# Add and GELU on one core: the first load of y cut into a narrow and a wide piece

## The chip, the cores and the metric

The kernel runs on one core of one Trainium2 chip. The metric is the device time of one execution in microseconds (us). The kernel before takes 120.14 us (median of three runs, 120.08 to 120.14).

## The reference

```python
batch, dim = 1024, 4096            # x and y, float32
z = x + y
out = 0.5 * z * (1 + tanh(sqrt(2/pi) * (z + 0.044715 * z**3)))   # float32
```

Each of x, y and the output has 16.78 MB, so 33.55 MB are read from HBM (the chip's main memory) and 16.78 MB are written to it. Nothing is used twice.

## The kernel before, in words

Each of the three tensors is seen as 128 partitions by 32768 columns (`xv`, `yv`, `ov`, L91). One partition holds eight whole rows of the tensor, which lie together in HBM, so a DMA over a range of columns moves one unbroken run of bytes per partition: 8192 columns make a run of 32 KB, 16384 columns one of 64 KB. In what follows such a run is called a row of the DMA.

Tile `z` (L120) holds all 32768 columns. The loads of x land in it, the sums overwrite them, the results overwrite the sums, and the stores leave from it. Loads of y go to tiles `y` of 8192 columns (`YS`), of which two buffers exist (`pool_y`, L115; taken in L131); a third y load must wait until the first buffer was read. `load_y` works out from a load's first column which tile it belongs to and where in it, and takes a new buffer only where that place is 0 (L129 to L131), so several loads may fill one tile.

The columns are worked on in 16 chunks of 2048 (`CH`). For chunk c there are four steps:

- `add` (L149): z = x + y, on VectorE (DVE) for chunks 0, 2, 4, 6, 8 and 12, on GpSimd (POOL) for the other ten.
- `mag` (L154): w = |z|, ScalarE (ACT), into one of two PSUM tiles.
- `gelu` (L157): w = gelu(-w), ScalarE.
- `end` (L166): z = max(z, 0) + w, VectorE.

All DMAs are issued by SyncE (SP), from one queue in a fixed order (L173):

```python
sp = [(load_y, 0), (load_x, 0), (load_y, 1), (load_x, 1), (load_y, 2), (load_y, 3)]
sp += [(store, i) for i in range(len(stores))]
```

The sizes, in columns, are `xloads = [16384, 16384]`, `yloads = [8192] * 4` and `stores = [16384, 10240, 6144]` (L96 to L99). The tile framework puts a wait in front of an issue where data or buffers ask for it: y load 2 waits for the adds of chunks 0 to 3, y load 3 for those of chunks 4 to 7, each store for the `end` steps of its columns. The first four loads wait for nothing.

`begin_early(nc, 2)` (L214) takes the first two DMAs of SP's queue and puts them ahead of the barrier with which the program starts; what stands behind them is issued after that barrier. `wait_late` (L215) rearranges the program's end so that the last store's completion is waited for late.

Of the kernel before, what the change touches and what calls it, by code (L numbers as in the profile page):

```python
# [66 lines left out]
def kernel(  # L67
# [26 lines left out]
    CH = 2048  # L94
    PS = 2
    xloads = [16384, 16384]  # L96
    yloads = [8192, 8192, 8192, 8192]
    FIRST = 8
    stores = [16384, 10240, 6144]  # L99

# [69 lines left out]
            ends.setdefault(c, ins.ins)  # L170


    sp = [(load_y, 0), (load_x, 0), (load_y, 1), (load_x, 1), (load_y, 2), (load_y, 3)]  # L173
    sp += [(store, i) for i in range(len(stores))]
    pool = [(add, c) for c in range(C) if c not in by_dve]
    dve, acts = [], []
# [69 lines left out]
```

## Time and profile before

| | |
|---|---|
| median of three runs | 120.14 us |
| span of the profiled execution, first to last instruction | 118.57 us (the page rounds to 118.6) |
| what lies around the span (120.14 less 118.57) | 1.57 us |
| DVE, ACT, POOL busy | 59.8, 60.8, 55.5 us (50, 51, 47%) |
| DMA packets' time, share of 16 engines' span | 98.6% |
| bytes moved | 50.33 MB, 424 GB/s over the span |
| first DMA issued; last DMA landed | 0.00 us; 118.53 us |

The page has no time of its own for the profiled execution besides the span; the table sets the span beside the median of the runs. The trace also records each DMA packet with its start, duration and size. A packet here is one row of a DMA; each of the 16 DMA engines carries 8 of the 128 rows of every DMA, and after them a packet of 4 bytes that counts up the semaphore.

### The profile page before, as it was taken

Reading aid. Unit: us, or ns where it says so; the run is one execution under the profiler, and the core shown is the slowest. Engines: PE = TensorE matmul, PEld = TensorE weight load, DVE = VectorE, ACT = ScalarE, POOL = GpSimd, SP = SyncE. Lnnn points to the kernel's source line nnn. Section 1 sums busy time; section 2 is a strip of 40 time slices with the busy share of each in tenths; the row PEclk is TensorE's granted clock in tenths of the full one; section 3 lists DMA queues with packets and bytes.
Section 4 is the critical chain, followed back from the end, with each engine's and each line's share of the span. In section 5 each row is a group of like instructions: output and inputs, shape, how many; then the busy total and the mean of one; then the engine's idle time right before and its main releaser. Section 6 shows DMA issues by size and latency. Waiting matters only on the chain.

```text
span 118.6 us, 160 instructions
## 1 busy us (share of the span) xinstructions
DVE 59.8 (50%) x24; ACT 60.8 (51%) x34; POOL 55.5 (47%) x14
## 2 busy tenths in 40 slices
DVE  0000000000399999699994594257999457742000
ACT  5000000000067979999379705797798999940000
POOL 0000000000399999997000029999999999100000
DMA  7989888998889988988899898998899889999996
GB/s 243 464 365 696 354 354 354 663 398 354 354 387 497 531 354 354 707 354 354 354 420 464 365 520 354 531 531 354 354 531 531 354 354 442 442 442 442 398 398 265
DMA packets 1296, 50.33 MB, mean 424 GB/s; under 512 B 144, under 2 KB 144, under 8 KB 144
## 3 DMA queue, kind: packets, MB, share of 16 engines
q1 hardware_dynamic: 1296, 50.33, 98.6%
HBM read 33.55 MB, written 16.78 MB: 424 GB/s over the span
## 4 chain that ended last, share of the span: by engine, by line
DMA 48%; POOL 34%; POOLq 4%; ACT 3%; DVE 2%; issue 0%; SPq 0%; DVEq 0%
POOL z L149 34%; DMA z<-in_x_dram 26%; DMA y<-in_y_dram 21%; POOLq L213 4%; DVE z L166 2%; ACT w L154 2%; ACT w L157 2%; SPq L132 0%; POOLq L149 0%; DVEq L166 0%
## 5 line engine op out<-in xcount | busy, mean ns | idle before, releaser
L149 POOL TENSOR_TENSOR z<-z,y 128x2048 f32<-128x2048 f32 x10 | 55.3, 5563 | 45.6 <-DMA z<-in_x_dram 31.1
L154 ACT ACTIVATE w<-z 128x2048 f32<-128x2048 f32 x16 | 30.1, 1880 | 42.5 <-DVE z L149 36.0
L166 DVE SCALAR_TENSOR_TENSOR z<-z,w 128x2048 f32<-128x2048 f32 (+1 forms) x17 | 36.4, 2157 | 16.0 <-ACT w L157 16.0
L149 DVE TENSOR_TENSOR z<-z,y 128x2048 f32<-128x2048 f32 x6 | 24.0, 4009 | 30.3 <-DMA z<-in_x_dram 30.1
L157 ACT ACTIVATE w<-w 128x2048 f32<-128x2048 f32 x16 | 29.8, 1862 | 0.5
L198 ACT ACT_TABLE_LOAD x1 | 1.3, 1283 | 1.3 <-PEq L230 1.3
L197 DVE MEMSET one<- 128x1 f32 x1 | 0.1, 59 | 1.3 <-PEq L230 1.3
L198 ACT ACTIVATE one<-one 128x1 f32<-128x1 f32 x1 | 0.2, 203 | 0.0
L230 POOL MEMSET const-float32-0.0<- 128x1 f32 x1 | 0.1, 98 | 0.2 <-issue 0.2
L230 POOL MEMSET const-bfloat16-1.0<- 128x1 bf16 x1 | 0.1, 101 | 0.0
L230 POOL MEMSET const-uint8-127<- 128x1 uint8 x1 | 0.1, 101 | 0.0
L230 POOL MEMSET const-float32-1.0<- 128x1 f32 x1 | 0.1, 98 | 0.0
## 6 DMA issues: line engine op xcount, KB each, us to landing
y<-in_y_dram SPq DMA_DIRECT2D x4, 4096.0 KB, 23.7
out_dram<-z SPq DMA_DIRECT2D x1, 5120.0 KB, 14.9
out_dram<-z SPq DMA_DIRECT2D x1, 3072.0 KB, 11.0
z<-in_x_dram SPq DMA_DIRECT2D x2, 44.9
out_dram<-z SPq DMA_DIRECT2D x1, 21.6
```

The source lines that it names most:

```text
L149: eng.tensor_add(out=zt[:, a:b], in0=zt[:, a:b], in1=yt[s][:, o : o + b - a])
L154: nc.scalar.activation(out=wt[c], in_=zt[:, a:b], func=act.Abs)
L157: nc.scalar.activation(out=wt[c], in_=wt[c], func=act.Gelu_apprx_tanh, scale=-1.0)
L166: ins = nc.vector.scalar_tensor_tensor(out=zt[:, a + o : a + o + n], in0=zt[:, a + o : a + o + n], scalar=0.0, in1=wt[c][:, o : o + n], op ...
L197: nc.vector.memset(one, 0.0)
L198: nc.scalar.activation(out=one, in_=one, func=act.Gelu_apprx_tanh)
L213: tc.compile()
L230: nc = _bacc.Bacc("TRN2", target_bir_lowering=False, num_devices=1)
```

## The change

The first load of y is made in two DMAs. The first carries columns 0 to 1023 (4 KB in each of 128 partitions, 0.5 MB), the second columns 1024 to 8191 (28 KB each, 3.5 MB). Both fill the same y tile. The order of the list on SP's queue stays otherwise the same; the other loads of y are numbered one higher.

```diff
     xloads = [16384, 16384]
-    yloads = [8192, 8192, 8192, 8192]
+    yloads = [1024, 7168, 8192, 8192, 8192]
     FIRST = 8
...
-    sp = [(load_y, 0), (load_x, 0), (load_y, 1), (load_x, 1), (load_y, 2), (load_y, 3)]
+    sp = [(load_y, 0), (load_y, 1), (load_x, 0), (load_y, 2), (load_x, 1), (load_y, 3), (load_y, 4)]
     sp += [(store, i) for i in range(len(stores))]
```

`begin_early(nc, 2)` is not changed. The two DMAs that it moves ahead of the barrier were the first y load and the first x load; now they are the two pieces of the first y load, and the first x load is issued behind the barrier. On the other engines every instruction stays, in the same order.

## The prediction

> **What bounds the kernel.** I read the page's DMA rows first, then the chain of waits, then the opening by windows and by the trace's single DMA packets.
>
> ```profile
> DMA  7989888998889988988899898998899889999996
> DMA packets 1296, 50.33 MB, mean 424 GB/s; under 512 B 144, under 2 KB 144, under 8 KB 144
> q1 hardware_dynamic: 1296, 50.33, 98.6%
> ```
>
> The 16 DMA engines are taken for 98.6% of the span, and no compute engine for more than 51%. The records of single packets say it more sharply: I followed each engine's 72 rows from the first to the last, and from one packet's end to the next one's start there is never more than 1 ns. The kernel is one unbroken DMA stream, so its end is the start of that stream, plus each engine's 3 MB at a fixed rate, plus a tail (the last packet ends at 118.07 us on the latest engine, the last semaphore counts at 118.53).
>
> The chain of waits shows why the compute work doesn't matter here although it names POOL for 34%:
>
> ```profile
> 0.43 30.92 DMA z<-in_x_dram
> ...
> 44.68 25.46 DMA y<-in_y_dram
> ```
>
> The 25.46 us of the third y load are mostly time behind the second x load, which lands at 60.4 us. SP issues every later DMA while an earlier one still moves: y load 2 at 44.7 us (x until 60.4), y load 3 at 57.9 (y load 2 until 70.1), the stores at 77.6, 96.3 and 107.6, with the DMA ahead landing at 79.9, 99.2 and 111.3. The smallest cover is 2.2 us, in front of the first store.
>
> So only two things can move the end: the time the stream takes per row, and its opening. The opening by windows (columns: busy time of DVE, ACT, POOL, granted clock, DMA share, GB/s; a packet is booked where it starts):
>
> ```profile
> 0.00:1.00 1.00, 0.00 (x0) 0.00 (x0) 0.20 (x4) 1.00 0.00 0
> 1.00:2.00 1.00, 0.06 (x1) 0.74 (x1) 0.00 (x0) 1.00 1.64 524
> 2.00:3.00 1.00, 0.00 (x0) 0.74 (x2) 0.00 (x0) 1.00 0.61 262
> 3.00:11.00 8.00, 0.00 (x0) 0.00 (x0) 0.00 (x0) 1.00 0.99 426
> ```
>
> 524 GB/s for 1 us are sixteen 32 KB rows, one per engine; a share of 1.64 means that they take 1.64 us on average. The next eight (262 GB/s) take 0.61 x 16 / 8 = 1.22 us, and in steady flow a row takes 1.21. The single records: first packets start between 1.019 and 1.951 us and take 2.135 (the earliest) to 1.214 us (the two latest, at 1.898 and 1.951). They end between 2.77 and 3.16. So the early starters lose up to 0.92 us in their first packet, the latest lose nothing, and each engine stays in the phase it then has. Second packets take 1.224 us on average, the worst 1.259; third ones 1.212.
>
> **The change, part by part.**
>
> *Eight more rows per engine.* The spacing of like packets is 908.3 ns for 24 KB, 1209.2 for 32 KB and 1510.3 for 40 KB. The slope is (1510.3 - 908.3) / 16384 = 0.03674 ns a byte, which leaves 908.3 - 903.0 = 5.3 ns per packet whatever its size. A row of 4 KB is then 155.8 ns, one of 28 KB 1058.8, together 5.3 more than one of 32 KB; eight rows make 43 ns. The extra DMA also adds one semaphore packet, 6 ns to the next packet's start. Sum in steady flow: +0.05 us. Nothing hides it, since the stream has no gaps.
>
> *The same in the opening.* All of the 4 KB rows run before about 3.2 us, where packets are slower. How a row of 4 KB behaves there no row shows. The lower end is the 5.3 ns of steady flow. The upper end for a switch to a fresh row is the worst second packet, 1.259 against 1.213: 46 ns. The mean excess of second packets is 1.224 - 1.213, 11 ns; but the end belongs to the slowest of 16 engines, not to the average. I take for that engine half of its eight switches at the worst and half at the mean: 4 x 46 + 4 x 11 = 228 ns. With the 49 ns above it is +0.28 us; the ends are +0.05 and 8 x 46 + 49 = +0.42 us.
>
> *Can the opening get shorter?* Shortening the first packet helps engines that lose time in it. But the engine that starts at 1.951 loses nothing (1.214 us against 1.213), and it alone carries the end: 1.951 plus the same 3 MB. A gain needs that latest start to move. The bound is the mean start of the 16 engines, 1.369 us: -0.58 us. A loss needs the slow flow to last: if the last engine ran its 32 KB of small rows as slowly as the slowest first packet, 2.135 instead of 1.214, that is +0.92 us.
>
> *The second piece of y behind the first.* It is issued where the first x load was, at 0.43 us. From issue to the engines the first DMA takes 1.02 to 1.95 us. With the same lag the second is 0.43 us behind the first on each engine, and the first piece keeps an engine busy for 8 x 0.156 = 1.25 us; 0.8 us to spare. If its lag is greater by more than that, the engines stand idle for the rest.
>
> *The first x load behind the barrier.* It takes the place of y load 1, at 1.26 us instead of 0.43; y load 1 and x load 1 move back by one issue (0.33 to 0.45 us), so the last of them ends by about 2.5 us. The first y tile keeps the engines busy to 11.24 us, so this costs nothing; without that cover it would be the 0.83 us of the later issue. Nothing else stands on SP between them, and POOL, DVE and ACT first wait for x at 31 us.
>
> *Waits.* The adds of chunk 0 now need two y semaphores instead of one, and y load 2's reuse of the buffer follows both; the x load that lands last (31.35 us, y at 12.0) still ends the wait. Behind that wait on SP stand y load 3 and the stores. If the stream moves, all of it moves alike, and the 2.2 us of cover stay.
>
> One rule speaks against a small DMA. The Trainium skill, "DMA: Bandwidth & Descriptors", section "Anatomy of one DMA — SWDGE (gpsimd) path", gives about 2.0 us fixed for each DMA; were it paid in the stream, the sum by it would be near 122.1 us. The trace differs: from the first y load's last row to the first x load's first row an engine loses 6 ns, so between queued DMAs such a cost isn't in the stream.
>
> The sum: 118.57 us of span + 0.28 + 1.57 around it = 120.42 us, against the median of 120.14. About 0.2% (0.24 us) is what a measurement of this kernel can tell from no change; the line runs through this forecast's band.
>
> **The rivals.**
>
> *Bookkeeping only, not slower.* The opening slows by time, not by row: all first packets end within 0.39 us of each other however early they began, which speaks for a common moment until which flow is thin. Then 32 KB in eight pieces meet the same moment as 32 KB in one, and only 0.05 to 0.15 us come on top: 120.19 us. Against it: second packets are still slow, by up to 46 ns, after that moment.
>
> *Faster.* The late starters are late because the early ones' long first packets stand before them. The spread of 0.93 us in starts, while only 16 rows flow, speaks for it; against it, the two latest run at full rate at once, beside engines that are at their slowest, and the number of rows in the first DMA stays at 128. If the latest start falls to between 1.6 and 1.37 us, the gain is 0.30 to 0.53 after the 0.05 of bookkeeping: 119.75 us at its middle. It decides from a latest start under 1.66 us.
>
> *Much slower.* The small rows are too short to cover what the opening asks of each fresh row, or the second piece reaches the engines late. Price between 0.42 and 0.97 us, in the middle 120.84 us. For it: the slowest first packet. Against it: the 0.8 us to spare, and the first x rows, fresh too, at 2.418 us like all later ones.
>
> *The change doing nothing* isn't a case of its own: two DMAs for one are in the program's order on SP.
>
> **How the numbers follow.** The forecast (+0.15 to +0.42) has 0.40, of which 0.12 falls under the line of 0.24 us and 0.28 over it. Bookkeeping only has 0.20, all of it the same. Faster has 0.24. Much slower has 0.16. So faster 0.24, same 0.12 + 0.20 = 0.32, slower 0.28 + 0.16 = 0.44. The range goes from 119.70, which leaves out the larger gains (about 0.08), to 120.95, which leaves out the larger losses (about 0.08) and leaves little for cases that I don't see. The forecast's own band is 120.29 to 120.56.
>
> **What would show it.** In the changed kernel's packets: sixteen rows of 4 KB starting near 1.02 to 1.95 us, as first rows did; on the latest engine, eight of them in about 1.48 us (8 x 0.156 + 0.23); no gap before the 28 KB rows; the first x row starting 0.28 us later than 11.25 to 11.65; and from there every landing later by the same amount. If the first x rows start within 0.1 us of before, the rival of bookkeeping holds; if earlier, the faster one; if there is a gap in front of the 28 KB rows, their late arrival. The forecast is wrong as a whole if the stream opens a gap anywhere behind the first x load, or if the time moves while the first x rows do not.

## The result, and the profile after

The changed kernel took 120.33 us (median of 21 runs, 120.12 to 120.64) against 120.12 us of the kernel before (21 runs beside it): ratio 1.0018, 95% interval 1.0011 to 1.0025. That is +0.21 us, against +0.28 forecast. Two later comparisons of the same code, on two chips, gave 0.9986 (0.9971 to 1.0001) and 0.9983 (0.9969 to 0.9997). By the medians those two differ from the kernel before by 0.04 and 0.07 us only; their ratios lie lower because 7 of the 29 and 7 of the 35 runs of the kernel before beside them took over 120.45 us, and none of the changed kernel's 12 and 12 did. The sign of so small a change did not hold from one set of runs to the next, and most of what follows rests on traces, where steps of 0.05 us within one trace can be seen.

The profiled run of the changed kernel took 120.16 us with a span of 118.67 us, 0.10 us over the span before. The page's DMA rows:

```profile
DMA  6999888998889988988899898998899889999996
DMA packets 1440, 50.33 MB, mean 424 GB/s; under 512 B 160, under 2 KB 160, under 8 KB 288
q1 hardware_dynamic: 1440, 50.33, 98.7%
```

There are 144 packets more (128 rows and 16 semaphore packets), the same bytes, and the stream is as full as before. The opening by windows, with the columns as before:

```profile
0.00:1.00 1.00, 0.00 (x0) 0.00 (x0) 0.20 (x4) 1.00 0.06 4
1.00:2.00 1.00, 0.06 (x1) 0.75 (x1) 0.00 (x0) 1.00 0.82 131
2.00:3.00 1.00, 0.00 (x0) 0.73 (x2) 0.00 (x0) 1.00 1.28 516
3.00:11.00 8.00, 0.00 (x0) 0.00 (x0) 0.00 (x0) 1.00 1.03 443
```

From 1 to 2 us 131 GB/s are 32 rows of 4 KB, which take 0.82 x 16 / 32 = 0.41 us on average, though one costs 0.156 in steady flow. Where only whole 32 KB packets could be seen before, the small rows now show when the opening is slow. By the trace's packets, sixteen first rows start between 0.996 and 1.702 us and take up to 1.031 us; rows that start between 2.0 and 2.5 us take 174 ns on average, and from 2.5 us on every one takes 159 (a packet's duration overlaps the next one's by 3). The 28 KB rows follow without a gap.

The chain of waits:

```profile
1.25 30.24 DMA z<-in_x_dram
...
44.85 25.42 DMA y<-in_y_dram
```

x load 0 is now issued at 1.25 us instead of 0.43 and still takes its turn in the stream; it lands at 31.49 instead of 31.35. From there every load lands 0.11 to 0.14 us later than before (41.20, 60.55, 70.27, 79.98), and the last store 0.10 us later (118.64).

### The profile page after: what moved, and what is told of

The parts are those of the page before. It is cut to its first block, busy times and chain, and to the rows that moved or that the text cites. A ratio compares the mean times of both kernels' runs of the same rounds, so it can differ in the third digit from the quotient of the medians.

```text
span 118.7 us, 162 instructions
## 1 busy us (share of the span) xinstructions
DVE 59.8 (50%) x24; ACT 60.8 (51%) x34; POOL 55.5 (47%) x14
## 4 chain that ended last, share of the span: by engine, by line
DMA 47%; POOL 34%; POOLq 4%; ACT 3%; DVE 2%; issue 0%; DVEq 0%
POOL z L149 34%; DMA z<-in_x_dram 25%; DMA y<-in_y_dram 21%; POOLq L213 4%; DVE z L166 2%; ACT w L154 2%; ACT w L157 2%; POOLq L149 0%; DVEq L166 0%
```

## The experiments

Theories: **switches** (the prediction's: each change to a fresh row costs extra while the opening is slow), **moment** (its first rival: the opening is slow until some moment, whatever the rows), and **order** (x load 0 behind the barrier is what costs). The edits are against the kernel before, where the heading doesn't name the changed kernel. The time shown is the median; the ratio is that to the kernel before on the same chip. It compares all runs of the two and lies near the ratio of their means, so it can differ from that of the medians by up to 0.15%.

**The changed kernel again.**

> The changed kernel once more, for a second trace of its opening. The theory of the prediction (every switch to a fresh row costs extra while the opening is slow): ratio 1.0015 to 1.0025, and 4 KB rows after an engine's first one that are visibly longer than 156 ns. The rival (the opening is slow until a moment, whatever the size of the rows): only an engine's rows before about 2 us are long, all later ones 156 ns, and the time is 0.05 to 0.15 us over the kernel before.

120.08 us, ratio 0.9986 (0.9971 to 1.0001). The slow-down didn't come back. In the trace only 4 of the 4 KB rows that start after 2 us take over 170 ns, and none that starts after 2.3 us, as *moment* has it. x load 0 lands at 31.43 us, 0.08 us later than in the first trace of the kernel before. The spread among engines is new: they have moved the first 32 KB between 2.50 and 3.26 us, where the kernel before needed 2.77 to 3.17. Most engines run ahead; the latest does not.

**The wide piece first.**

```diff
+    yloads = [7168, 1024, 8192, 8192, 8192]
+    sp = [(load_y, 0), (load_y, 1), (load_x, 0), (load_y, 2), (load_x, 1), (load_y, 3), (load_y, 4)]
```

> The same two pieces in the other order: 28 KB rows first, then 4 KB rows. The first x load still stands behind the barrier, and the number of rows and DMAs is that of the changed kernel. Theory (small rows cost in the opening): the small rows now run at about 10 us, so +0.05 us, ratio 1.0004. Rival (slow until a moment): +0.05 us as well. Third theory (it is the x load behind the barrier, or the second piece's issue, that costs): as the changed kernel, +0.2 us, ratio 1.0018.

120.18 us, 1.0001 (0.9982 to 1.0021): no cost to be told, which speaks against *order* at 1.0018, though the interval just reaches it. x load 0 lands at 31.49 us, as in the changed kernel, although the small rows now run at 10 us. That speaks against *switches*. The profiled execution took 120.56 us, and its landings show where the extra time sits: from x load 1 to the y load behind it 9.85 us pass and to the next one 9.89, against 9.70 and 9.72 in the kernel before. Summed over the rows that start from 35 to 82 us, an engine loses 0.57 us here against steady rows, and 0.06 in the first trace of the kernel before. That has nothing to do with the edit, as the later copies show.

**The split in the second tile.**

```diff
+    yloads = [8192, 1024, 7168, 8192, 8192]
+    sp = [(load_y, 0), (load_x, 0), (load_y, 1), (load_y, 2), (load_x, 1), (load_y, 3), (load_y, 4)]
```

> The split is made in the second load of y instead of the first; the first two DMAs are those of the kernel before. It has the rows and the semaphores of the changed kernel, but away from the opening: what the stream pays for rows alone. All theories: 8 x 5.3 + 6 ns, +0.05 us, ratio 1.0004. If it is as slow as the changed kernel (1.0018), the opening has no part in the cost.

120.15 us, 1.0002 (0.9985 to 1.0019). The trace gives the price far better than the time: from x load 0's landing to that of the split tile 41.171 - 31.400 = 9.771 us pass, against 9.726, 9.722 and 9.723 us in three traces of the kernel before. The split costs the stream +0.047 us in this one trace; 0.049 had been worked out. The same stretch without a split takes 9.705 to 9.726 us over all traces that have it, so the price is good to some 0.02 us.

**Eight small pieces in the first tile.**

```diff
+    yloads = [1024] * 8 + [8192, 8192, 8192]
+    sp = [(load_y, 0), ..., (load_y, 7), (load_x, 0), (load_y, 8), (load_x, 1), (load_y, 9), (load_y, 10)]
```

> The first tile of y is loaded by eight DMAs of 4 KB rows: 64 rows per engine instead of 8, and seven more DMAs. By the stream's own price 64 x 155.8 + 8 x 6 less 8 x 1209.2 + 6 ns: +0.34 us, ratio 1.0028. Rival (slow until a moment): just that. Theory (a switch costs extra in the opening): the first eight or sixteen of an engine's rows carry 0.23 us on top, +0.57 us or more, ratio 1.0047. If DMAs of small rows can't be issued as fast as they are carried out (1.25 us each), gaps show between them and the loss is greater.

121.83 us, 1.0132 (1.0107 to 1.0158): +1.6 us (120.12 x 0.0132; 1.7 by the medians), beyond all theories. The windows show where:

```profile
3.00:4.00 1.00, 0.00 (x0) 0.00 (x0) 0.00 (x0) 1.00 1.06 406
4.00:5.00 1.00, 0.00 (x0) 0.00 (x0) 0.00 (x0) 1.00 0.87 287
5.00:6.00 1.00, 0.00 (x0) 0.00 (x0) 0.00 (x0) 1.00 0.97 344
```

The eight DMAs land at 3.42, 4.65, 7.19, 8.47, 9.81, 11.12, 12.41 and 13.67 us. All spacings but one are 1.23 to 1.34 us; the third DMA takes 2.54. That is 1.29 us over the 1.25 of steady flow (8 x 0.156 + 0.006), and so most of what the eight cost beyond the 0.34 us worked out. It is the first one behind the barrier, issued at 1.26 us. From 4.0 to 4.5 us only 12.1 of the 16 engines have a packet in flight on average: some stand idle, over 2.7 us after that issue. So the prediction's last means of getting slower, a piece that reaches the engines late, is real; in the changed kernel it had no chance, since 28 KB rows stand behind the small ones. Rows of 200 to 1060 ns show until about 10.5 us, beside which SP was issuing until 7.5 us. Why the third DMA reaches the engines so late is not shown.

**The same eight in the second tile.**

```diff
+    yloads = [8192] + [1024] * 8 + [8192, 8192]
+    sp = [(load_y, 0), (load_x, 0), (load_y, 1), ..., (load_y, 8), (load_x, 1), (load_y, 9), (load_y, 10)]
```

> Eight DMAs of 4 KB rows again, now for the second tile of y, whose rows run at 31 to 41 us; the first two DMAs are those of the kernel before. In the first tile these eight cost 1.58 us instead of the 0.34 worked out from the steady stream. If that is the opening and the issues beside it, the second tile pays the stream's price, +0.34 us, ratio 1.0028, and all its rows take 156 to 160 ns. If rows of 4 KB in a longer row cost that much anywhere, ratio 1.013 again, and rows of 200 to 400 ns show among them.

120.63 us, 1.0037 (1.0024 to 1.0050). By the trace the tile lands 41.703 - 31.478 = 10.225 us after x load 0, +0.50 us against 9.724. That is more than the 0.34 of the steady price: 391 of the 1024 small rows take 160 to 219 ns instead of 159, which makes 0.14 us an engine. But it is less than a third of what the same eight cost in the opening. So the rest of their 1.6 us belongs to the opening and the issues beside it, not to 4 KB rows as such. Why a third of the rows are late here is open.

**x load 0 early again, in the changed kernel.**

```diff
-    begin_early(nc, 2)
+    begin_early(nc, 3)
```

> The changed kernel with three DMAs ahead of the barrier instead of two, so that the first x load is issued early again, right behind the two pieces of y. If the x load behind the barrier is part of the cost, the time falls from 1.0018 towards 1.0004. Theory of the prediction and the rival of a slow moment: no change against the changed kernel, 1.0005 to 1.0025, since the first tile of y covers the issue to 11 us; the barrier itself falls some 0.4 us later, which nobody waits for.

120.08 us, 1.0003 (0.9992 to 1.0015). x load 0 is issued at 0.89 us and lands at 31.45, inside the 31.43 to 31.49 of the changed kernel's three traces. *Order* falls: 0.36 us of earlier issue brought the landing no nearer.

**x load 0 before y load 0.**

```diff
+    sp = [(load_x, 0), (load_y, 0), (load_y, 1), (load_x, 1), (load_y, 2), (load_y, 3)]
```

> The kernel before with its first two DMAs exchanged: 64 KB rows of x first, then 32 KB rows of y. Rows, bytes and DMAs are the same, so the opening alone tells. Slow until a moment: ratio 1.0000, within 0.0005, and the first rows' excess over 2.418 us is as large as it was over 1.213 us. If the excess of the opening grows with the size of the first rows, up to 0.4 us slower (1.003); if fewer switches in the opening help, up to 0.1 us faster.

120.25 us, 1.0012 (0.9999 to 1.0025): by time, undecided. By trace, the first 12 MB have landed at 31.62 us instead of the 31.31 to 31.48 of the five traces that begin with an unsplit y load: the opening is some 0.25 us longer with 64 KB rows in front. So the size of the first rows is not without effect, and *moment* doesn't hold in its pure form; this is one trace.

**The first load split by partitions.**

```diff
-        nc.sync.dma_start(out=yt[s][:, o : o + b - a], in_=yv[:, a:b])
+        for p, q in ((0, 16), (16, P)) if i == 0 else ((0, P),):
+            nc.sync.dma_start(out=yt[s][p:q, o : o + b - a], in_=yv[p:q, a:b])
```

> The first load of y is split by partitions instead of columns: 16 partitions in a first DMA, so that each engine gets one 32 KB row of it, and the other 112 in a second. Rows are as many and as long as before; one semaphore packet more (6 ns). If the spread of the first rows' starts (1.02 to 1.95 us) comes from the 128 rows of the first DMA, the latest engine starts earlier and the time falls by up to 0.5 us, ratio 0.996. If it comes from a moment of the whole stream, ratio 1.0000 within 0.0005. If the 112 rows don't spread evenly over 16 engines, some engines carry more and the end is later by a row, 1.2 us (1.01).

129.91 us, 1.0803 (1.0779 to 1.0826): +9.6 us. None of the outcomes expected fits. The first rows start from 1.03 to 1.86 us, so one row per engine makes the starts no closer. The cost is elsewhere. In the third trace of the kernel before the window from 1 to 2 us reads

```profile
1.00:2.00 1.00, 0.06 (x1) 0.74 (x1) 0.00 (x0) 1.00 1.82 524
```

and with the split by partitions:

```profile
1.00:2.00 1.00, 0.06 (x1) 0.75 (x1) 0.00 (x0) 1.00 3.71 524
2.00:7.00 5.00, 0.00 (x0) 0.73 (x2) 0.00 (x0) 1.00 0.61 105
7.00:12.00 5.00, 0.00 (x0) 0.00 (x0) 0.00 (x0) 1.00 1.00 269
12.00:19.00 7.00, 0.00 (x0) 0.00 (x0) 0.00 (x0) 1.00 1.02 257
24.00:40.00 16.00, 0.00 (x0) 0.00 (x0) 0.00 (x0) 1.00 0.97 420
```

The sixteen first rows take 3.71 us on average, and the rows of the 112 partitions run at 257 to 269 GB/s until they are through at 22.0 us; with all 128 partitions again the stream is back at its rate. All engines are busy the whole time. The rows are as many and as long as before; what differs is which partitions the engines write side by side. That this is the cause is argued, not shown.

**Halves.**

```diff
+    yloads = [4096, 4096, 8192, 8192, 8192]
+    sp = [(load_y, 0), (load_y, 1), (load_x, 0), (load_y, 2), (load_x, 1), (load_y, 3), (load_y, 4)]
```

> The first tile of y in two halves of 16 KB rows: as many rows and semaphores as the changed kernel, but a first row four times as long. Rival (slow until a moment): as the changed kernel, 0.05 to 0.15 us, ratio 1.0004 to 1.0012. Theory of the prediction (a cost for each switch in the opening): only one or two switches fall into it, 0.05 to 0.1 us, ratio 1.0004 to 1.0008. In the trace the engines have moved their first 32 KB between 2.7 and 3.25 us either way.

120.16 us, 0.9998 (0.9983 to 1.0013); x load 0 lands at 31.49 us. 16 KB rows in front do what 4 KB and 28 KB rows did. *Switches* asked for less here than in the changed kernel, and there is no difference.

**The kernel before against itself, twice.**

> The kernel before against itself: ratio 1.0000, and the interval shows what such a comparison can tell. Its trace is a second look at the opening: if the latest engine's first row ends again at 3.16 us the opening is the same in each execution, otherwise its scatter is part of the scatter of the times.

> The kernel before against itself, the measure for the run beside it: ratio 1.0000, within 0.001. In the trace the first x load lands at 31.31 to 31.40 us, as in three traces so far, and the rows that run late lie between 40 and 80 us, by anything from 0 to 0.6 us an engine.

120.10 us, 0.9993 (0.9981 to 1.0005), and 120.15 us, 0.9999 (0.9980 to 1.0019). The opening repeats: the latest engine has moved 32 KB at 3.19 and 3.16 us (3.17 in the first trace), and x load 0 lands at 31.31 and 31.32. The first of the two traces has a run of 120.24 us, the second one of 120.00, and the difference is in the middle: an engine loses 0.34 and 0.04 us in rows that start from 35 to 82 us. With 0.57 us in the run of 120.56, 0.37 in the one with x in front (120.40) and 0.05 to 0.10 in five runs of 120.09 to 120.16, this is where much of the scatter between executions comes from, though not all: the run of the halves has 0.08 at 120.28. Why those rows are late is open.

**The changed kernel a third time.**

> The changed kernel a third time, on whatever chip this call gets, beside the kernel before as a kernel of its own. If the 1.0018 of the first comparison is the change's, it comes back here within 1.0008 to 1.0028; if it was the scatter between loads of the programs, the ratio lies between 0.999 and 1.001, and the trace shows the first x load landing 0.08 to 0.15 us later than before all the same.

120.04 us, 0.9983 (0.9969 to 0.9997), beside 120.15 us for the copy of the kernel before. Again no loss; the median is 0.07 us under that of the kernel before (120.11). The trace has the loss that the others have: x load 0 at 31.43 us, the last store's landing at 118.58 (118.53, 118.72 and 118.48 in the kernel before).

## Why the prediction was right, and where it was not

**The bound** held: one DMA stream without gaps, in which a shift of x load 0 travels to the end. Compute, waits and barrier had no part in it.

**Rows and semaphore in steady flow** held: 49 ns worked out, 47 measured in the second tile, where traces differ by some 20.

**Switches in the opening** is the term that was mis-sized. I gave it 0.23 us. The chain's line for x load 0 (issue, time to landing) reads, in three traces of the kernel before, in the runs with the split and with the eight in the second tile, and in three traces of the changed kernel:

```profile
0.43 30.92 DMA z<-in_x_dram
0.43 30.88 DMA z<-in_x_dram
0.43 30.89 DMA z<-in_x_dram
0.43 30.97 DMA z<-in_x_dram
0.42 31.05 DMA z<-in_x_dram
1.25 30.24 DMA z<-in_x_dram
1.25 30.18 DMA z<-in_x_dram
1.26 30.18 DMA z<-in_x_dram
```

The five traces with an unsplit first tile have x load 0 landing at 31.353, 31.313, 31.323, 31.400 and 31.478 us, mean 31.373; six with a split one at 31.490, 31.433, 31.434, 31.446, 31.488 and 31.486, mean 31.463. The difference is 0.09 us, and 0.05 of it is the steady price: 0.04 us is left for the opening, no more than the traces differ among themselves. Like against like, three traces of the changed kernel (mean 31.452) against three of the kernel before (31.330), it is 0.12 us, and 0.07 is left. How to choose matters, since the two unsplit traces that land last (31.400 and 31.478) are those in which SP has more DMAs to issue in the opening: five and eight by 4.1 us, against four in the kernel before and five in the changed one. Their second and third rows are longer too, 1.231 and 1.222 us in the first, 1.244 and 1.233 in the second, against 1.220 to 1.227 and 1.212 to 1.213. So the one issue more is a rival for what is left, and no run here separates it from the short rows.

The 4 KB rows show why 0.23 was too much. As the price of a switch, the excess that I read from second packets (11 ns on average, 46 at worst) should stand on every small row of the opening. But of the changed kernel's small rows in its first trace, the 52 that start from 2.5 us on all take 159 ns, just what all 128 take at 10 us in the run with the wide piece first. The long ones are the early ones, and they pass the same slow time in which one 32 KB row stood before. What made the second packets long stays open. By the sign that I had set, the first x row of the latest engine, the first trace of the changed kernel lies between the forecast and the rival of bookkeeping (11.78 us, against 11.63 to 11.66 in three traces before), and the two later ones, at 11.74 and 11.72, are within 0.1 us of before. The rival of bookkeeping only (+0.05 to +0.15) describes the traces.

**No gain in the opening** held in the traces, but not for the reason given. I had said that the engine that starts last, at 1.951 us, loses nothing and alone carries the end, so that a gain needs that start to move. It moved, and nothing was gained. In the first trace of the changed kernel the last engine to start, at 1.702 us, runs its small rows at full rate and is through them at 2.95; the engine that is through last, at 3.30 us, had started at 1.358 and lost its time in its first three rows (436, 420 and 314 ns). In the run with the eight in the second tile, whose first tile is not split, all first rows start by 1.263 us, and still the last one ends at 3.28 (3.17 in the kernel before). So the latest start does not set the end of the opening. In two traces of the changed kernel x load 0's first rows start on average at 11.27 and 11.34 us, earlier than the 11.46 to 11.49 of the three traces before, and that is no gain either: the latest starts at 11.74 and 11.72 against 11.63 to 11.66, and a load has landed only when the latest engine is through.

**The second piece and x load 0** cost nothing, as said: there is no gap in front of the 28 KB rows, and the issue at 0.89 instead of 1.25 us changes nothing. But 0.8 us to spare rested on a lag that I took to be the same for each DMA; the third of eight small ones needed over 2.7 us.

**The skill's rule** was no rival to the sum. The Trainium skill, "DMA: Bandwidth & Descriptors", section "Anatomy of one DMA — SWDGE (gpsimd) path", gives its fixed 2.0 us for DMAs that GpSimd issues, and says that waiting for the completion makes up most of it. Here SyncE issues all DMAs, and one more cost 0.047 us in the trace where it was queued behind others.

**The total.** 120.42 forecast and 120.33 measured are close, but not by the step that made the difference; that closeness is luck. The profiled executions have +0.10 us of span, about the loss at x load 0; the other half of the +0.21 in the first comparison appears in no trace here, and the two later comparisons don't have it. Whether chip, placement or chance made it is open. What is shown is a loss of 0.09 to 0.12 us at x load 0, of which 0.05 is the steady price. It is under the 0.2% that a measurement can tell: the kernel before against itself gave intervals from 0.9980 to 1.0019. Two figures of the rivals are slips that the sum doesn't use: the middle of the faster one is 119.73 us, and 120.19 is the lower end of bookkeeping, not its middle.

## What to carry to other kernels

In a kernel that is one unbroken DMA stream, price a split by the row: here 5.3 ns for each row more on an engine and 6 ns for the semaphore, and check it with the landings of neighbouring DMAs in one trace, which here agreed to 0.02 us where medians don't resolve tenths. Look for the engine that is through last, not for the mean and not for the one that starts last, since a landing waits for it. Keep at least one long DMA behind a short one at the start, and never split such a load by partitions to save time without measuring it.

## What the runs showed of the hardware

- The opening is a slow stretch of the whole stream more than a cost of its first rows: in the first trace of the changed kernel 4 KB rows took up to 1.03 us when they started near 1 us, 174 ns on average from 2.0 to 2.5 us, and 159 after that. With 32 KB rows the last first row ended at 3.17 us when the starts reached to 1.95 us, and at 3.28 when all were made by 1.26. With 64 KB rows in front the first 12 MB landed some 0.25 us later (one trace).
- A DMA issued at 1.26 us behind two others left engines idle at 4.0 to 4.5 us, although in the kernel before the first DMA of all reached its engines 1.02 to 1.95 us after its issue.
- The same 128 rows of 32 KB, given out as 16 and 112 partitions, ran at 257 to 269 GB/s once the second of the two was under way, and cost 9.6 us. The Trainium skill, "DMA: Bandwidth & Descriptors", section "The descriptor swizzle", describes a transfer over 128 partitions in which each engine writes one port of its own; this run fits with that order being lost, but does not show the ports.
- Much of the difference between executions stands in rows that start from 35 to 82 us: 0.04, 0.06 and 0.34 us an engine in three traces of the kernel before, 0.57 in the run with the wide piece first, with nothing in the edits that explains it.
